# Sixteen tokens' expert rows gathered for the first expert product of a mixture layer

## The chip, the cores and the metric

The kernel runs on one core of a Trainium2 chip. The metric is the device time of one execution in microseconds (us), as the median of several runs. The engines are TensorE (PE; its weight loads are listed as PEld), VectorE (DVE), ScalarE (ACT), GpSimd (POOL) and SyncE (SP), which here issues nearly all transfers. Each engine works through its own queue in order.

## The reference

The whole is a network of four layers on 256 tokens of width 1024, in float32: two layers with attention, convolution and a gated FFN, one with an mLSTM mixer, one with stick-breaking attention. The last two each end in the expert layer (`peer_ffn`), which is what the change touches:

```
q = xb @ w_q                                  # 8 heads x 2 halves x 128
s = q . sub_keys; s_top, i_top = top_k(s, 16) # 128 keys per half
cand = all 16 x 16 sums; g_top, pos = top_k(cand, 16)
expert = i_top[0][..] * 128 + i_top[1][..]    # 16 of 16384 experts per head and token
act = gelu(einsum('thkd,td->thk', take(peer_u, expert), xb))
out = einsum('thk,thkd->td', softmax(g_top) * act, take(peer_v, expert))
```

`peer_u` and `peer_v` are 16384 x 1024 each, per layer. A token uses 128 of the 16384 experts. Its input is xb = normalised x times (1 + scale) plus shift.

## The kernel before

**Split products.** Every large product is made of three matmuls in a reduced float32 format. A weight of 128 x 1024 is loaded by SP (`raw`, four buffers), rounded by ScalarE (`whi`, L177), and the remainder is made by VectorE or POOL (`wlo`, L180); `whi` and `wlo` have five buffers each. `mm3` (L185 to L187) multiplies hi by hi, hi by lo and lo by hi.

**The expert layer** (`peer`, L896) is computed densely. The 16384 experts are 128 chunks of 128, and there are two products per chunk. `up(c)` multiplies a chunk of `peer_u` with the activations h (1024 x 256, one column per token): 8 x 3 = 24 matmuls of 256 columns into `pA`, then a Gelu by ScalarE (L920) into a table of activations. `down(c)` multiplies the weighted activations with a chunk of `peer_v`: 12 matmuls of 512 columns into `acc`. Between them `weigh` (L954) multiplies the table by each token's routing weights: it builds one-hot tables on VectorE (L961, L962, L967) and forms the dense weights by 16 f16 matmuls of 64 columns (`pG`, L971) for eight tokens and half of the chunks, and VectorE multiplies these into the table (L979).

**The order of the work.** Chunks 0 to 63 of `up` carry the routing beside them (`route`): for each of two blocks of 128 tokens first eight steps of top 16 among the keys, then four among the candidates, then four groups of one-hot operations (L1130, L1133, L1135; two of each) that look up the chosen keys. In chunks with c divisible by 3 (22 per layer) POOL makes the lo half, in the others VectorE. Chunks 64 to 99 of `up` carry `weigh` for the first half of the chunks; the last 28 chunks of `up` alternate with the first 28 of `down`, the next `down` chunks carry the other half of `weigh`, and the rest run alone. The order within an engine is set when the program is built: a scheduler puts the instructions in order by the written sequence, by data and by constraints that the code sets, such as `issue_after`, which holds a piece of work until a named instruction has been placed.

**What the layer's stream x does meanwhile.** Two tiles `x[0]` and `x[1]` of 128 x 1024 hold the network's residual stream in SBUF. In the expert layer they are only needed at its end, where `gated_x` adds the result to them. The tile `xa1` of a normalised block is free after the activations are transposed, and holds `wr`, the split activations of `down`.

## Time and profile before

| | |
|---|---|
| median of 3 runs | 2894.22 us (2889.6 to 2897.99) |
| the profiled execution | 2893.22 us, span 2891.4 us |
| mean granted TensorE clock | 0.996 of full speed |
| busy, share of the span | PE 98%, PEld 89%, DVE 75%, ACT 50%, POOL 5% |
| transfers | 543.42 MB, mean 188 GB/s |

The two expert layers start their first `up` chunk at 1093.6 us and 2095.6 us of the span. A busy engine in the profile executes or holds an instruction; matmuls are pipelined, so what counts for TensorE is the distance between starts, not the duration of one. The bracket at the end of a timeline row is the idle time before it and what ended it; where a wait is for several things, the one that came last by the profile is named.

### The profile page before, as it was taken

The numbers are of one execution on the slowest core, as the hardware profiler recorded it, in microseconds if no ns is written. First come the engines' busy times: TensorE is split into PE (matmuls) and PEld (weight loads), VectorE is DVE, ScalarE is ACT, GpSimd is POOL, SyncE is SP. The second block draws the span as 40 slices with busy tenths as digits, with TensorE's granted clock in tenths as the row PEclk, the third lists the DMA queues.
The fourth block names the chain that finished last, engine by engine and source line by source line (L and its number), as shares of the span: only waits on it lengthen the run. The fifth ranks groups of instructions, "written<-read, shape, count | busy, mean of one in ns | idle before, by whom it ended". The sixth has DMA issues, their size and how long they took to land.

```text
span 2891.4 us, 50436 instructions
## 1 busy us (share of the span) xinstructions
PE 2846.0 (98%) x19669; PEld 2575.9 (89%) x19669; DVE 2168.8 (75%) x4178; ACT 1442.9 (50%) x2372; POOL 144.2 (5%) x54
## 2 busy tenths in 40 slices
PE   8999999999999999999999999999999999999999
PEld 7998997999997889989999887877899999988887
DVE  6986766886755859968866997686599787569865
ACT  6645445654545854443344344567544434443454
POOL 0000000000000003320000000000033100000000
PEclk9999999999999999999999999999999999999999
DMA  6485775376666455554687358653455545554564
GB/s 210 135 280 191 265 247 190 111 250 221 235 192 186 161 169 163 173 197 139 196 279 254 117 193 284 217 180 101 146 163 182 170 139 166 186 165 131 186 201 146
DMA packets 153713, 543.42 MB, mean 188 GB/s; under 512 B 20018, under 2 KB 21250, under 8 KB 153346
## 3 DMA queue, kind: packets, MB, share of 16 engines
q1 hardware_dynamic: 153474, 540.20, 57.9%
q8 instruction: 154, 2.52, 0.4%
q14 instruction: 85, 0.70, 0.1%
HBM read 539.04 MB, written 1.09 MB: 187 GB/s over the span
## 4 chain that ended last, share of the span: by engine, by line
PE 86%; DVE 11%; ACT 1%; DMA 1%; issue 1%; SPq 0%; DVEq 0%; ACTq 0%
PE acc L185 8%; PE acc L187 8%; PE acc L186 8%; PE mmB L185 7%; PE mmB L186 7%; PE mmB L187 7%; PE pA L185 5%; PE pA L186 5%; PE pA L187 5%; PE mmA L185 5%; PE mmA L186 5%; PE mmA L187 5%; PE pG L971 4%; DVE wlo L180 3%; PE sc L193 1%
## 5 line engine op out<-in xcount | busy, mean ns | idle before, releaser
L177 ACT CAST whi<-raw 128x1024 fp32r<-128x1024 f32 x893 | 935.8, 1050 | 872.1 <-PE pA L186 358.2
L180 DVE TENSOR_TENSOR wlo<-raw,whi 128x1024 fp32r<-128x1024 f32 x849 | 1049.7, 1241 | 344.3 <-ACT whi L177 341.0
L185 PE MATMUL pA<-hhi,whi 128*128 128x256 f32 x2048 | 586.7, 286 | 10.6 <-ACT act L920 9.5
L186 PE MATMUL pA<-hlo,whi 128*128 128x256 f32 x2048 | 579.8, 283 | 0.0
L187 PE MATMUL pA<-hhi,wlo 128*128 128x256 f32 x2048 | 579.6, 283 | 0.0
L185 PE MATMUL mmB<-hhi,whi 128*128 128x256 f32 x1480 | 422.0, 285 | 0.0
L186 PE MATMUL mmB<-hlo,whi 128*128 128x256 f32 x1480 | 420.2, 284 | 0.0
L187 PE MATMUL mmB<-hhi,wlo 128*128 128x256 f32 x1480 | 419.9, 284 | 0.0
L185 PEld LDWEIGHTS pA<-hhi,whi 128*128 128x128 f32 x2048 | 394.2, 192 | 15.1 <-ACT act L920 11.4
L187 PE MATMUL acc<-whi,wr 128*128 128x512 f32 x1024 | 400.4, 391 | 0.8 <-DVE wr L992 0.5
L186 PE MATMUL acc<-wlo,wr 128*128 128x512 f32 x1024 | 401.0, 392 | 0.0
L186 PEld LDWEIGHTS pA<-hlo,whi 128*128 128x128 f32 x2048 | 393.1, 192 | 2.2
L185 PE MATMUL acc<-whi,wr 128*128 128x512 f32 x1024 | 393.2, 396 | 0.0
L187 PEld LDWEIGHTS pA<-hhi,wlo 128*128 128x128 f32 x2048 | 392.8, 192 | 0.0
L185 PEld LDWEIGHTS mmB<-hhi,whi 128*128 128x128 f32 x1480 | 282.8, 191 | 1.8
L187 PEld LDWEIGHTS mmB<-hhi,wlo 128*128 128x128 f32 x1480 | 282.8, 191 | 0.6
L186 PEld LDWEIGHTS mmB<-hlo,whi 128*128 128x128 f32 x1480 | 282.9, 191 | 0.5
L991 ACT CAST wr<-act 128x256 fp32r<-128x256 f32 x256 | 103.5, 406 | 343.7 <-PE acc L186 338.3
L187 PEld LDWEIGHTS acc<-whi,wr 128*128 128x128 f32 x1024 | 192.3, 188 | 44.9 <-DVE wr L992 4.8
L186 PEld LDWEIGHTS acc<-wlo,wr 128*128 128x128 f32 x1024 | 192.6, 188 | 39.2 <-DVE wlo L180 0.6
L185 PEld LDWEIGHTS acc<-whi,wr 128*128 128x128 f32 x1024 | 193.1, 189 | 35.7
L542 DVE CUSTOM_DVE_ANT_0 adaw<-adaw,cb 128x1024 f32<-128x1024 f32 x112 | 136.8, 1222 | 78.4 <-DMA adaw<-in_ada_w 74.7
(353 smaller groups left out, 4037.4 us busy)
## 6 DMA issues: line engine op xcount, KB each, us to landing
raw<-in_peer_u SPq DMA_DIRECT2D x256, 512.0 KB, 3.8
raw<-in_peer_v SPq DMA_DIRECT2D x256, 512.0 KB, 4.3
adaw<-in_ada_w SPq DMA_DIRECT2D x96, 512.0 KB, 4.5
raw<-in_w_gates SPq DMA_DIRECT2D x80, 512.0 KB, 3.7
raw<-in_w_down SPq DMA_DIRECT2D x44, 512.0 KB, 4.0
raw<-in_w_gate SPq DMA_DIRECT2D x36, 512.0 KB, 3.8
raw<-in_w_up SPq DMA_DIRECT2D x36, 512.0 KB, 3.8
raw<-in_w_qkv SPq DMA_DIRECT2D x24, 512.0 KB, 4.5
```

Of the source, the lines that this page charges most:

```text
L177: (nc.vector.tensor_copy if FIRST_HI[i:i + 1] == "v" else nc.scalar.copy)(hi, raw)
L180: self.last_lo = lo_eng.tensor_tensor(lo, raw, hi.bitcast(F32), op=ALU.subtract)
L185: nc.tensor.matmul(out, lhsT=lhs[0], rhs=rhs[0], start=start, stop=False)
L186: nc.tensor.matmul(out, lhsT=lhs[0], rhs=rhs[1], start=False, stop=False)
L187: return nc.tensor.matmul(out, lhsT=lhs[1], rhs=rhs[0], start=False, stop=stop)
L193: self.nc.tensor.matmul(out, lhsT=lhs[a], rhs=rhs[b], start=start and i == 0, stop=stop and i == 2)
L542: nc.vector.tensor_tensor_reduce(w, w, self.csilu, 1.0, 0.0, op0=ALU.mult, op1=ALU.add, accum_out=col[:, j:j + 1])
L971: nc.tensor.matmul(pg[:, :, 4 * g + t], lhsT=e2[:, g, :, t], rhs=e1[:, j, :, t], start=(j == 0), stop=(j == 1))
L991: nc.scalar.copy(gh, row(c))
```

## The change

The first `TG` = 16 tokens are left out of the dense first product: `up` runs on 240 columns. For these tokens the 128 expert rows of each token are gathered from `peer_u` (given a second time as plain rows, `peer_u_rows`) by 16 indirect transfers per layer, issued by POOL into `x[0]` and `x[1]` in turn, 128 rows of 4 KB each: gather j fetches one expert for each of 8 groups of 16 tokens' places. VectorE multiplies a gathered tile with `xg` (the 16 tokens' activations repeated eight times, with the shift added) and sums along the row (`dot`). After the last one the results are turned, passed through Gelu, multiplied by the routing weights, transposed and split into three bf16 parts `gP`; in `weigh` the own tokens use `gP` in place of the routing weights (24 matmuls instead of 16), and ScalarE writes the result where the others multiply it into the table.

x is saved to two DRAM tiles before, and read back at chunk 97 of `down`. The sixteen gathers are due at chunks 32, 35, 39, 42, 46, 49, 53, 56, 60, 63, 67, 70, 74, 77, 81 and 84, the dot of each three chunks later. The own tokens' `weigh` is last among the calls for the first half. NA falls from 100 to 98, so 30 chunks of `up` and `down` alternate. The one-hot lookups of the routing are made in f16 with the heads last: four groups per layer of six operations, the widest over 2048 elements, instead of eight.

```diff
-        N1, NA, FIN, GATE, TAIL = 64, 100, 58, 110, 4
+        N1, NA, FIN, GATE, TAIL = 64, 98, 58, 110, 4
+        G0, G1 = 32, 88
...
             def up(c, dst, lo_eng=None):
                 w = self.split_w(d["peer_u"][l, c], lo_eng=lo_eng)
-                p = self.pa.tile([128, S], F32, tag="sc", name="pA")
+                p = self.pa.tile([128, S - TG], F32, tag="sc", name="pA")
                 for k in range(KD):
-                    mm = self.mm3(p, [v[:, k * 128:(k + 1) * 128] for v in w], [v[:, k, :] for v in h],
+                    mm = self.mm3(p, [v[:, k * 128:(k + 1) * 128] for v in w], [v[:, k, TG:S] for v in h],
                                   k == 0, k == KD - 1)
-                return mm, nc.scalar.activation(dst, p, AF.Gelu)
+                return mm, nc.scalar.activation(dst[:, TG:S], p, AF.Gelu)
+
+            xd = [self.dram.tile([128, D], F32, name=f"xd{t}{l}") for t in range(NT)]
+
+            def gather_setup():
+                xg = self.np.tile([128, D], F32, tag="xa1", name="xg")
+                nc.sync.dma_start(xg, shift)
+                for t in range(NT):
+                    nc.sync.dma_start(xd[t], self.x[t])
+                fg = self.x[0]
+                for g in range(NG):
+                    nc.sync.dma_start(fg[g * TG:(g + 1) * TG, :], norm.xa[0][0:TG, :])
+                nc.vector.tensor_tensor(xg, xg, fg, op=ALU.add)
+                return xg
+
+            def gather_places():
...
+                nc.vector.tensor_scalar(eu, gw[:, 0], float(l * 16384), None, op0=ALU.add)
+                for g in range(NG):
+                    nc.sync.dma_start(gidx[g * TG:(g + 1) * TG, :], eu[:, g * TG:(g + 1) * TG])
+
+            def gather(j):
+                r = self.x[j % 2]
+                nc.gpsimd.indirect_dma_start(out=r, out_offset=None, in_=d["peer_u_rows"],
+                                             in_offset=bass.IndirectOffsetOnAxis(ap=gidx[:, j:j + 1], axis=0))
+                return r
+
+            def dot(j, r):
+                nc.vector.tensor_tensor_reduce(r, r, xg, 1.0, 0.0, op0=ALU.mult, op1=ALU.add,
+                                               accum_out=dots[:, j:j + 1])
+
+            def gather_end():
...
+                p = self.pt.tile([128, TG], F32, tag="tp", name="tpg")
+                nc.tensor.transpose(p, gw[:, 0], self.ident[0:TG, 0:TG])
...
+            for j in range(TG):
+                turn.setdefault(G0 + j * (G1 - G0) // TG, []).append(j)
+
+            def gathers(c):
+                if c == G0 - 4:
+                    assert pks
+                    gather_places()
+                for j in turn.get(c - 3, ()):
+                    with tc.issue_after(self.last_lo.ins):
+                        dot(j, got.pop(j))
+                for j in turn.get(c, ()):
+                    assert len(got) < 2
+                    got[j] = gather(j)
+                if c == G1 + 2:
+                    assert not got
+                    gather_end()
...
             for c in range(64):
                 mark = up(c, act1[:, c, :], nc.gpsimd if c % 3 == 0 else nc.vector)
...
+                if c == 4:
+                    xg = gather_setup()
+                gathers(c)
...
             for c in range(64, NA):
                 up(c, row(c), nc.vector)
-                while done < 32 and done * (NA - 65) < (c - 63) * 32:
-                    weigh(0, 8 * done)
+                gathers(c)
+                while done < 32 and done * (NA - 65) < (c - 63) * 32 and (done < (S - TG) // 8 or c >= NA - 3):
+                    weigh(0, (8 * done + TG) % S)
                     done += 1
...
-            for hg in range(4):
-                hs = slice(2 * hg, 2 * hg + 2)
-                oh = [B.tile([128, 2, 16, 16], F32, tag=f"oh{i}", name="oh") for i in range(2)]
-                for i in range(2):
-                    nc.vector.tensor_tensor(oh[i], bc(af[:, i, hs, :, None], [128, 2, 16, 16]),
-                                            bc(io16[:, None, None, :], [128, 2, 16, 16]), op=ALU.is_equal)
-                for i in range(2):
-                    nc.vector.tensor_tensor(oh[i], oh[i], bc(fi[:, hs, i, None, :], [128, 2, 16, 16]), op=ALU.mult)
-                for i in range(2):
-                    nc.vector.tensor_reduce(pk[:, i, hs, :], oh[i], axis=AX.X, op=ALU.add)
+            for i in range(2):
+                oh = B.tile([128, 16, 16, 8], F16, tag="oh", name="oh")
+                nc.vector.tensor_tensor(oh, bc(af[:, i, None], [128, 16, 16, 8]),
+                                        bc(self.iota8[:, :, None, :], [128, 16, 16, 8]), op=ALU.is_equal)
+                nc.vector.tensor_tensor(oh, oh, bc(fi[:, i, :, None, :], [128, 16, 16, 8]), op=ALU.mult)
+                for n in (8, 4, 2):
+                    nc.vector.tensor_tensor(oh[:, 0:n], oh[:, 0:n], oh[:, n:2 * n], op=ALU.add)
+                nc.vector.tensor_tensor(pk[:, i].rearrange("p h s -> p s h"), oh[:, 0], oh[:, 1], op=ALU.add)
                 yield 3.6
```

What the scheduler makes of it shows in two queues. The numbers at the names are those of buffers or of tiles, and `[waits ...]` are the semaphores that an instruction waits for: DMASW0 to DMASW7 count the gathers by turns, DMAHW the transfers of SP. VectorE's queue in the first expert layer, before, around chunks 36 and 37 (the lo half of chunk 35 is `wlo_13671`, that of 37 `wlo_13747`; that of 36 is POOL's):

```order
L180 TENSOR_TENSOR wlo_13671<-raw_13668,whi_13670 128x1024 [waits DMAHW4_49,PE_49,Activation_49]
L1049 MAX v_13390<-sc1_11712 128x8 x2
L1051 MAX_INDEX iu_13391<-v_13390,sc1_11712 128x8 [waits DVE_49] x2
L1053 MATCH_REPLACE sa_13700<-v_13390,sc1_11712 128x128
L1053 MATCH_REPLACE sa_13701<-v_13390,sc1_11712 128x128
L1055 MAX v_13390<-sa_13700 128x8 [waits DVE_49]
```

And the same place after (the lo half of chunk 35 is `wlo_13732`, of 37 `wlo_13798`, of 38 `wlo_13846`, of 40 `wlo_13912`; L960 is `dot`, whose second row reads the sum out):

```order
L183 TENSOR_TENSOR wlo_13732<-raw_13729,whi_13731 128x1024 [waits DMAHW6_49,PE_49,Activation_49]
L960 ISA x0_89,dots_11705<-x0_89,xg_12485 128x1024 [waits DMASW0_49]
L960 ISA dots_11705 128x1
L960 ISA x0_89,dots_11705<-x0_89,xg_12485 128x1024 [waits DMASW2_49]
L960 ISA dots_11705 128x1
L183 TENSOR_TENSOR wlo_13798<-raw_13795,whi_13797 128x1024 [waits DMAHW0_49,PE_49,Activation_49]
...
L183 TENSOR_TENSOR wlo_13846<-raw_13843,whi_13845 128x1024 [waits DMAHW1_49,PE_49,Activation_49]
L960 ISA x1_97,dots_11705<-x1_97,xg_12485 128x1024 [waits DMASW1_49]
L960 ISA dots_11705 128x1
L960 ISA x1_97,dots_11705<-x1_97,xg_12485 128x1024 [waits DMASW4_49]
L960 ISA dots_11705 128x1
L183 TENSOR_TENSOR wlo_13912<-raw_13909,whi_13911 128x1024 [waits DMAHW3_49,PE_49,Activation_49]
```

Between two lo halves there now stand two dots on the same tile, `x0` and then `x1`, each waiting for its own gather. POOL's whole queue, before, from the broadcasts of the first two layers on, holds one row of 22 lo halves for each expert layer:

```order
L292 TENSOR_SCALAR gb<-gb 128x1024 x4
L180 TENSOR_TENSOR wlo<-raw,whi 128x1024 x22
L774 MEMSET svz_21365 128x2048
L774 MEMSET svz_21366 128x2048
L180 TENSOR_TENSOR wlo<-raw,whi 128x1024 x22
```

and after, from the lo half of chunk 21 (`wlo_13137`) to that of chunk 42 (`wlo_14005`):

```order
L183 TENSOR_TENSOR wlo_13137<-raw_13134,whi_13136 128x1024 [waits PE_49,DMAHW0_49,Activation_49,Pool_49]
L955 DMA x0_89<-in_peer_u_rows,gidx_11704 128x1024 [waits DMAHW4_49,DMAHW5_49,DMAHW3_49,DMAHW6_49,DMAHW2_49,DMAHW7_49,DMAHW1_49,DMAHW0_49]
L955 DMA x1_97<-in_peer_u_rows,gidx_11704 128x1024
L183 TENSOR_TENSOR wlo_13248<-raw_13245,whi_13247 128x1024 [waits PE_49,Activation_49,Pool_49]
L183 TENSOR_TENSOR wlo_13380<-raw_13377,whi_13379 128x1024 [waits PE_49,DMAHW6_49,Activation_49,Pool_49]
L183 TENSOR_TENSOR wlo_13511<-raw_13508,whi_13510 128x1024 [waits PE_49,DMAHW1_49,Activation_49,Pool_49]
L183 TENSOR_TENSOR wlo_13652<-raw_13649,whi_13651 128x1024 [waits PE_49,DMAHW4_49,Activation_49,Pool_49]
L955 DMA x0_89<-in_peer_u_rows,gidx_11704 128x1024 [waits DVE_49] x2
L183 TENSOR_TENSOR wlo_13766<-raw_13763,whi_13765 128x1024 [waits PE_49,DMAHW7_49,Activation_49,Pool_49]
L955 DMA x1_97<-in_peer_u_rows,gidx_11704 128x1024 [waits DVE_49] x2
L183 TENSOR_TENSOR wlo_13879<-raw_13876,whi_13878 128x1024 [waits PE_49,DMAHW2_49,Activation_49,Pool_49]
L183 TENSOR_TENSOR wlo_14005<-raw_14002,whi_14004 128x1024 [waits PE_49,DMAHW5_49,Activation_49,Pool_49]
```

The first gathers into each tile stand ahead of the lo half of chunk 24; two more into `x0`, each waiting for VectorE, stand ahead of that of chunk 36 (`wlo_13766`), and two more into `x1` ahead of that of chunk 39. The second expert layer has the same pattern.

## Rows read from the trace of the kernel before

**Rows 1.** The page: busy us (share) xinstructions, then the chain of waits.

```profile
...
PE 2846.0 (98%) x19669; PEld 2575.9 (89%) x19669; DVE 2168.8 (75%) x4178; ACT 1442.9 (50%) x2372; POOL 144.2 (5%) x54
...
PE 86%; DVE 11%; ACT 1%; DMA 1%; issue 1%; SPq 0%; DVEq 0%; ACTq 0%
```

**Rows 2.** Windows, second expert layer: stretch, length, busy us by engine, PEclk, DMA.

```profile
...
2037.00:2095.60 58.60, 56.96 (x424) 53.21 (x424) 28.21 (x44) 32.71 (x62) 4.78 (x2) 1.00 0.51 161
2095.60:2143.00 47.40, 47.39 (x393) 47.31 (x394) 47.40 (x211) 22.75 (x33) 14.76 (x5) 1.00 0.50 154
...
2188.00:2237.00 49.00, 47.17 (x391) 46.74 (x389) 48.93 (x149) 20.82 (x31) 13.55 (x5) 1.00 0.54 181
2237.00:2284.60 47.60, 47.08 (x390) 46.82 (x391) 31.17 (x47) 25.79 (x42) 15.53 (x5) 1.00 0.61 196
...
2330.00:2376.00 46.00, 46.00 (x466) 45.53 (x465) 39.97 (x68) 16.04 (x24) 0.00 (x0) 1.00 0.45 138
```

**Rows 3.** Timeline of TensorE: start, duration, engine, line, operation, tiles, count.

```profile
...
1550.25 0.39 PE L187 MATMUL acc<-whi,wr 128*128 128x512 f32 x1
...
1552.30 0.39 PE L187 MATMUL acc<-whi,wr 128*128 128x512 f32 x1
...
1552.64 0.28 PE L186 MATMUL pA<-hlo,whi 128*128 128x256 f32 x1
...
1553.48 0.28 PE L187 MATMUL pA<-hhi,wlo 128*128 128x256 f32 x1
```

**Rows 4.** Timeline, all engines, at chunk 48, second expert layer; [idle before].

```profile
...
2233.32 1.28 DVE L1130 TENSOR_TENSOR oh<-af,iota 128x512 f32<-128x512 f32 x2
...
2236.08 1.04 ACT L177 CAST whi<-raw 128x1024 fp32r<-128x1024 f32 x1 [5.13 <-DMA raw<-in_peer_u]
2236.92 1.21 DVE L180 TENSOR_TENSOR wlo<-raw,whi 128x1024 fp32r<-128x1024 f32 x1
...
2237.46 0.19 PEld L185 LDWEIGHTS pA<-hhi,whi 128*128 128x128 f32 x1 [2.26 <-ACT act L920]
2237.46 0.39 PE L185 MATMUL pA<-hhi,whi 128*128 128x256 f32 x1 [2.06 <-ACT act L920]
```

**Rows 5.** Timeline of weight loads, eight of the scores in one row.

```profile
1052.35 0.97 PEld L1088 LDWEIGHTS pss<-sk,q 128*128 128x128 f32 x8 [0.15 <-ACT q L1075]
```

**Rows 6.** VectorE's instructions by shape: count, busy us, mean ns, idle before.

```profile
...
L542 DVE CUSTOM_DVE_ANT_0 adaw<-adaw,cb 128x1024 f32<-128x1024 f32 x112 | 136.8, 1222 | 78.4 <-DMA adaw<-in_ada_w 74.7 <-DMA adaw<-in_kv_ada_w 3.3
...
L961 DVE TENSOR_TENSOR e<-iota,slots 128x1024 f16<-128x1024 f16 x128 | 87.4, 683 | 1.5 <-ACT slots L1154 1.5
L962 DVE TENSOR_TENSOR e<-iota,slots 128x512 f16<-128x512 f16 x128 | 53.2, 417 | 0.0
...
L1133 DVE TENSOR_TENSOR oh<-oh,fi 128x512 f32<-128x512 f32 x32 | 31.6, 1025 | 0.0
```

**Rows 7.** POOL's lo halves by shape, 1095 to 1285.

```profile
...
L180 POOL TENSOR_TENSOR wlo<-raw,whi 128x1024 fp32r<-128x1024 f32 x20 | 59.3, 2966 | 126.4 <-ACT whi L177 112.9 <-PE pA L186 13.6
```

**Rows 8.** Issues of transfers: KB each, median us to landing.

```profile
...
raw<-in_peer_u SPq DMA_DIRECT2D x256, 512.0 KB, 3.8
...
ab<-rowsd SPq DMA_DIRECT2D x5, 512.0 KB, 5.5
cb<-in_c SPq DMA_DIRECT2D x2, 512.0 KB, 7.4
```

**Rows 9.** Windows around an idle stretch of TensorE, first expert layer.

```profile
...
1256.00:1260.70 4.70, 0.00 (x0) 0.00 (x0) 1.23 (x2) 2.77 (x4) 0.00 (x0) 0.65 0.82 324
1260.70:1263.00 2.30, 2.29 (x10) 2.29 (x11) 1.38 (x2) 2.11 (x3) 0.00 (x0) 0.50 0.59 173
1263.00:1265.00 2.00, 2.00 (x14) 2.00 (x14) 1.91 (x2) 0.00 (x0) 0.00 (x0) 0.70 0.68 195
```

**Rows 10.** Timeline of TensorE, one chunk of the `weigh` stage.

```profile
...
2288.49 0.36 PE L185 MATMUL pA<-hhi,whi 128*128 128x256 f32 x1
...
2292.41 0.36 PE L185 MATMUL pA<-hhi,whi 128*128 128x256 f32 x1
```

More of the change, by code (lines that the diff above doesn't have):

```diff
@@ L904, in peer @@
             h = norm.h
-            wr = self.np.tile([128, 2, 2, S], F32R, tag="xa1", name="wr")
-            slots = P(ctx, "pea").tile([128, 4, S], F16, name="slots")
+            EA = P(ctx, "pea")
+            slots = EA.tile([128, 4, S], F16, name="slots")
+            gidx = EA.tile([128, TG], U32, name="gidx")
+            dots = EA.tile([128, TG], F32, name="dots")
+            gw = EA.tile([TG, 2, 128], F32, name="gw")
+            gP = EA.tile([128, 3, TG], BF16, name="gP")
             wI, wP = slots[:, 0:2], slots[:, 2:4]
@@ new lines, in gather @@
+            def gather(j):
[7 more added lines that the diff above has]
+            def gather_end():
+                for g in range(NG):
+                    nc.sync.dma_start(gw[:, 0, g * TG:(g + 1) * TG], dots[g * TG:(g + 1) * TG, :])
+                nc.scalar.activation(gw[:, 0], gw[:, 0], AF.Gelu)
+                nc.vector.tensor_tensor(gw[:, 0], gw[:, 0], gw[:, 1], op=ALU.mult)
+                p = self.pt.tile([128, TG], F32, tag="tp", name="tpg")
+                nc.tensor.transpose(p, gw[:, 0], self.ident[0:TG, 0:TG])
+                r = dots
+                nc.scalar.copy(r, p)
+                for j in range(3):
+                    nc.vector.tensor_copy(gP[:, j], r)
+                    if j < 2:
+                        nc.vector.tensor_tensor(r, r, gP[:, j], op=ALU.subtract)
@@ L925, in spare @@
                     self.pop()
-            steps, ends = self.route(rctx, l, sc, wI, wP)
+            steps, ends, pks = self.route(rctx, l, sc, wI, wP)
             took = 0
+            got = {}
+            turn = {}
+            for j in range(TG):
[13 more added lines that the diff above has]
+                    gather_end()
             for c in range(64):
@@ L956, in weigh @@
                 pg = self.pt.tile([128, 64, 8], F32, tag="tp", name="pG")
-                e2 = B.tile([128, 2, 128, 4], F16, tag="e2", name="e2")
-                e0 = B.tile([128, 2, 64, 4], F16, tag="e0", name="e0")
+                own = t0 < TG
+                dt = BF16 if own else F16
+                parts = [gP[:, j] for j in range(3)] if own else [wP[:, j] for j in range(2)]
+                e2 = B.tile([128, 2, 128, 4], dt, tag="e2", name="e2")
+                e0 = B.tile([128, 2, 64, 4], dt, tag="e0", name="e0")
                 tg = lambda a, n: bc(a.rearrange("p (g t) -> p g t", t=4)[:, :, None, :], [128, 2, n, 4])
@@ L978, in weigh @@
                     v = tl[:, r0:r0 + i1 - i0, t0:t0 + 8]
-                    nc.vector.scalar_tensor_tensor(v, pg[:, i0:i1, :], 1.0 / WSCALE, v, op0=ALU.mult, op1=ALU.mult)
+                    if own:
+                        nc.scalar.activation(v, pg[:, i0:i1, :], AF.Copy, scale=1.0 / WSCALE)
+                    else:
+                        nc.vector.scalar_tensor_tensor(v, pg[:, i0:i1, :], 1.0 / WSCALE, v, op0=ALU.mult, op1=ALU.mult)
             acc = []
@@ L1027, in peer @@
                     C = P(ctx, "pec", 2)
+                    for t in range(NT):
+                        nc.sync.dma_start(self.x[t], xd[t])
                 if c == GATE:
@@ L1162, in route @@
         pks = []
-        return (u for t in range(NT) for u in start(t)), [lambda t=t: end(t, pks[t]) for t in range(NT)]
+        return (u for t in range(NT) for u in start(t)), [lambda t=t: end(t, pks[t]) for t in range(NT)], pks
 def layout(inp):
@@ L1309, in body @@
     kv = ada.pop(1)
-    norms += [Late(0, ada[0], 0), Late(2, ada[0], 24), Late(4, kv, 0), Late(7, ada[1], 24)]
+    norms += [Late(0, ada[0], 0), Late(2, ada[0], 24), Late(5, kv, 0), Late(8, ada[1], 24)]
     net.first_layer(1, norms[1], norms[2])
@@ L1314, in body @@
     net.bg = later
-    net.peer(0, norms[3], lambda: row(3), norms[4])
+    net.peer(0, norms[3], lambda: row(3), norms[4], row(4))
     assert not net.bg
-    net.shared_kv_sb(norms[4], (row(5), ada[1][:, 0:KD]), row(6), norms[5])
-    net.peer(1, norms[5], lambda: row(8), None, out)
+    net.shared_kv_sb(norms[4], (row(6), ada[1][:, 0:KD]), row(7), norms[5])
+    net.peer(1, norms[5], lambda: row(9), None, row(10), out)
 def kernel(**inputs):
```

51 lines of the change are left out of this document (32 added, 19 removed).

## Prediction

> **What bounds the kernel now.** I read the page first: TensorE is busy for 2846.0 us of a span of 2891.4 and holds 86% of the chain of waits, VectorE is busy 75% of the span and holds 11% of the chain [rows 1]. An average hides the stages, so next came the stretches of the second expert layer [rows 2]. In the first 48 chunks, while the routing runs, VectorE is busy for 47.40 of 47.40 us at their start and 48.93 of 49.00 at their end: it is full, and TensorE with 47.39 and 47.17 waits little yet. From chunk 48 (2237 us) on, VectorE has room (31.17 of 47.60), and in the stage with `weigh` it is at 39.97 of 46.00 while TensorE is at 46.00 of 46.00. So TensorE sets the pace from chunk 48, and VectorE before it. Third came the spacing of the matmuls in the timeline [rows 3]: nine steps of 512 columns take 2.05 us, 228 ns each; seven steps of 256 columns take 0.84 us, 120 ns each. A chunk's 24 matmuls are therefore 2.88 us. Last, how a late VectorE reaches TensorE [rows 4]: VectorE puts a one-hot group (2233.32 to 2236.92) ahead of a lo half; the raw buffers come free by lo halves, so ScalarE's cast at 2236.08 has waited 5.13 us for a raw load, the Gelu behind it is late, and TensorE has waited 2.06 us for that Gelu at 2237.46. There is no slack for more VectorE work, or VectorE waiting, ahead of chunk 48.
>
> All that follows is per expert layer, of which there are two, against the profiled execution of 2893.2 us (1.0 below the median of 2894.2).
>
> **The gain: 240 columns.** From 228 ns and 120 ns a column costs (228 - 120)/256 = 0.42 ns, so 16 columns less are 6.7 ns, a step of 113.3 ns, and 24 of them save 0.16 us a chunk. It counts only where TensorE sets the pace: chunks 48 to 127, 80 x 0.16 = **-12.9 us**. Narrow f32 steps have one neighbour: eight products of 128 columns load their weights in 0.97 us [rows 5] with 0.19 us for one [rows 4], (0.97 - 0.19)/7 = 111 ns a step though they have half the columns. So the weight load, or whatever else sets that floor, would allow 113; the saving is bounded by 9 ns at best (0.22 us a chunk) and by nothing at worst, a step that stays at 120.
>
> The Trainium skill's page "TensorE: Matmul & The Clock Gate" (section on the back-to-back issue gap) says that in a stream of weight load and matmul pairs the spacing is set by both operations, not by the columns alone. The rows here bear out a floor of 111 ns at 128 columns, but contradict its sustained figure for 512 columns (about 131 ns; here 228). By its rule a step near the floor need not shrink, which is the third rival below.
>
> **VectorE's work up to chunk 47.** Before, five of the eight one-hot groups stand ahead of that chunk's lo half, at 3.60 us each (2233.32 to 2236.92) [rows 4], 18.0 us. After, four groups of f16 operations replace the eight, and all four stand ahead of it. For an f16 operation of 2048 elements there is no row; 512 and 1024 elements take 417 and 683 ns busy [rows 6], so each doubling adds about as much again: 1.2 us for 2048, and two of these with the halving adds come to about 3.6 us a group, 14.4. Bounds: 2.4 us a group if the wide ones run at half of that, 5 us if the wide strides cost as f32 does. New are four dot products: the nearest row is the 128x1024 multiply with accumulation of the ada stage, 1222 ns [rows 6], 1.3 us each with the read of the sum, 5.2. Sum -18.0 + 14.4 + 5.2 + 0.4 for the index arithmetic (two operations of 128 elements, each below the 417 ns for 512) = +2.0; VectorE's operations stretch beside POOL's (the one-hot products take 1025 ns on average [rows 6], while a whole group of six can end in 3.60 [rows 4]), so **+2.3** (-3 to +8). The other three groups that go stood after chunk 47, where VectorE has room, and are worth nothing.
>
> **The gathers: two full latencies on VectorE.** In VectorE's order two dots on the same buffer stand back to back after the lo half of chunk 35, and two more after that of chunk 38. The second of a pair reads a gather that overwrites what the first one reads, so POOL can issue it only when the first dot is done, and the second waits out the whole transfer while VectorE stands still. Behind it in VectorE's queue are the lo half of chunk 37 and the routing; on POOL, behind a third gather that waits for the second dot, is the lo half of chunk 36 that TensorE needs next. Nothing covers this: VectorE was full there. No gather by indices is in the trace. The nearest rows are transfers of 512 KB: 3.8 us for an expert chunk, 5.5 for the rows read back from DRAM, 7.4 for a slow one [rows 8]. I take 5.5, since a gather reads 128 scattered rows, not one block: 2 x 5.5 = **+11.0** (7.6 to 14.8). A third pair stands before chunk 58, where VectorE has had ten chunks of room (31.17 of 47.60), and is taken as hidden; uncovered it would be 5.5 more.
>
> The Trainium skill's page "DMA: Bandwidth & Descriptors" (anatomy of one DMA on the GpSimd path) gives 2.0 us plus the bytes at 436 GB/s, an estimate of 3.2 us for such a gather. No run here shows it; by that the two waits would be 6.4 instead of 11.0 and the whole forecast 9 us lower.
>
> **The clock.** After TensorE had stood still for 4.7 us and more it was granted 0.50 (1.2 of 2.4 GHz) and the next 24 matmuls took 4.3 us instead of 2.88 [rows 9]. The waits above leave gaps of that kind (a gather, a dot, and POOL's 3.0 us [rows 7] for chunk 36 or 39). One of the two falls where VectorE is late anyway: **+1.6** (0 to 3.2).
>
> **Smaller terms.** SP's eight small index transfers wait for VectorE ahead of the raw loads of chunks 25 on, four buffers deep: **+1.0** (0 to 3). A chunk of the `weigh` stage takes 3.92 us (2288.49 to 2292.41) [rows 10], in which VectorE has 3.41 us of work (39.97 of 46.00) [rows 2]; TensorE's part falls to 3.76, and seven dots over 24 chunks add 9.1 us against 24 x 0.35 = 8.4 of room: **+1.0** (0 to 3). The own tokens take 24 instead of 16 matmuls of 64 columns in four `weigh` calls; sixteen take 3.92 - 2.88 = 1.04 us, so 32 x 65 ns = **+2.1**. The own tokens' `weigh` waits for the last gathers at the turn to `down`: **+1.0** (0 to 3). Saving x to DRAM, loading xg and adding it stand in the stretch before chunk 0, where VectorE is busy 28.21 of 58.60 and the transfer engines 0.51 of it, and x comes back long before the end: 0 (without that cover up to 4 us).
>
> **Sum.** Per layer -12.9 + 2.3 + 11.0 + 1.6 + 1.0 + 1.0 + 2.1 + 1.0 = +7.1; for two, +14.2, or 2907. The forecast is **2907 us**, slower. With its costs near their ends, the case itself spans 2897 to 2922.
>
> **Rivals.**
> 1. *VectorE's routing becomes cheap enough to pay for short waits: faster.* With f16 groups of 2.4 us VectorE's sum by chunk 47 is -2.8 instead of +2.0, and with gathers of 3.8 us and no clock loss a layer comes to -12.9 - 2.8 + 7.6 + 2.1 + 1.0 = -5.0, in all 2883. If nothing stalled at all, TensorE would set the pace in all 128 chunks: -20.6 + 4 a layer, 2860. For it: f16 operations of 512 elements take 417 ns, the f32 products of the one-hot groups 1025 [rows 6]. Against it: the second dot of a pair cannot start earlier than the end of the first plus a transfer, however early the first is.
> 2. *Both halves cancel.* With 3.8 us a gather, no clock loss and the small terms at zero: -12.9 + 2.3 + 7.6 + 2.1 = -0.9 a layer, 2891. Only the shortest row for 512 KB speaks for it.
> 3. *The 240-column step stays at 120 ns.* The change then does not do what it says: 2 x 12.9 more, 2933. For it is the floor at 111 ns, against it that 113 is still above that floor.
> 4. *Products of fewer than 256 columns run at a lower rate in this number format.* No such row exists here in the format of the split weights; the 128-column f32 step of 111 ns speaks against it. At half the rate a step would be some 214 ns (12 + 2 x 101), 24 x 256 x 94 ns = +577 us.
>
> **How the numbers follow.** Forecast 0.41, rival 1 0.24, rival 2 0.23, rival 3 0.10, rival 4 0.02. About 0.3% (8.7 us) is what a measurement of this kernel can tell from no change. Faster by that is rival 1, 0.24; within it rival 2, 0.23; slower the forecast with rivals 3 and 4, 0.53. For 8 in 10 the range leaves out the lower third of rival 1, the upper half of rival 3, the tail of the forecast, and rival 4: 2872 to 2936.
>
> **What would show it.** In the profile after: pA steps of 113 ns; `x0<-in_peer_u_rows` landing 5 to 6 us after its issue; two idle stretches of VectorE of some 5 us released by a DMA within chunks 35 to 40 of each layer, and TensorE waiting there at a lo half of POOL's; chunk 48 starting about 157 us after chunk 0 (before: 2237.46 - 2095.6 = 141.9); chunks of 3.76 us in the `weigh` stage (before 3.92), and 5.46 where up and down alternate (before 2.88 and twelve steps of 228 ns, 5.62). The forecast is wrong if chunk 48 comes at less than 145 us after chunk 0, if the step is 120 ns, or if the `weigh` stage turns to VectorE's pace.

## The result: 3123 us, 7.9% slower, and the profile after

| | before | after |
|---|---|---|
| median (lowest to highest of 4 runs each, same chip) | 2893.72 us (2889.6 to 2897.99) | 3123.34 us (3117.56 to 3125.41) |
| ratio, 95% interval | | 1.0794 [1.0781, 1.0807] |
| span of the profiled execution, mean granted clock | 2891.4 us, 0.996 | 3123.6 us, 0.965 |

The sign was forecast, the size (+14 us) was not: the change costs +230 us. The page of the changed kernel, to be held beside [rows 1]:

```profile
span 3123.6 us, 50831 instructions
...
PE 2886.3 (92%) x19735; PEld 2591.6 (83%) x19735; DVE 2196.4 (70%) x4237; ACT 1443.3 (46%) x2388; POOL 162.2 (5%) x86
...
PE 71%; DVE 12%; DMA 9%; issue 4%; ACT 2%; SPq 1%; POOL 1%; DVEq 0%; ACTq 0%; POOLq 0%
```

VectorE is busy for 28 us more and TensorE for 40 (in the stretch below alone it is busy 50 us longer for the same matmuls, beside a granted clock of 0.82), but no engine is fuller than before. What has grown is the part of the chain that is no engine's work: DMA from 1% to 9%, issue from 1% to 4%. That points to queues that wait for each other. The windows say where. The rows read as in [rows 2]; first the start of the second layer and its `weigh` stage, then chunks 98 to 127 of the first and of the second layer, which hold the same work but for the ada product, VectorE's product with a transferred tile of weights of the next modulation (`adaw`), which only the first has:

```profile
2296.56:2355.60 59.04, 54.94 (x479) 54.05 (x480) 58.80 (x221) 26.59 (x40) 17.27 (x6) 1.00 0.46 150
...
2528.00:2575.00 47.00, 47.00 (x508) 46.62 (x507) 46.63 (x83) 17.25 (x26) 3.75 (x4) 1.00 0.59 176
...
1489.00:1787.00 298.00, 206.43 (x1045) 174.38 (x1044) 111.45 (x149) 77.08 (x116) 0.00 (x0) 0.82 0.46 148
2655.40:2812.00 156.60, 156.60 (x1046) 143.08 (x1045) 83.41 (x87) 77.59 (x117) 0.00 (x0) 1.00 0.64 195
```

298.00 against 156.60 us for the same matmuls: 141 us are lost in this one stretch, in which no engine is full. The rest shows in how late a chunk starts. The table gives, for the first / second layer, the start of a chunk counted from that layer's chunk 0, less the same in the kernel before (us). From chunk 64 to 100 some 5 us come into it that the end of the layer gives back, since `weigh` ends and `down` starts two chunks earlier (2.8 of them by chunk 98 in e7). Chunk 48 starts 172.8 / 173.2 us after chunk 0; the forecast had 157.

| kernel | c=24 | c=40 | c=48 | c=64 | c=98 | c=127 |
|---|---|---|---|---|---|---|
| after | 11.8 / 12.5 | 29.6 / 29.6 | 31.4 / 31.3 | 46.3 / 36.7 | 66.4 / 38.7 | 204.1 / 35.0 |
| ada product put back (e1) | 10.9 / 11.7 | 28.3 / 28.9 | 31.8 / 30.9 | 46.2 / 37.2 | 49.3 / 40.8 | 45.6 / 37.1 |
| three mends (e4) | 6.0 / 5.9 | 11.4 / 11.2 | 17.4 / 17.6 | 29.4 / 19.4 | 30.9 / 23.0 | 27.2 / 19.3 |
| routing alone (e7) | 2.4 / 2.2 | 3.9 / 3.6 | 5.8 / 5.0 | 0.6 / 4.9 | 3.4 / 7.8 | 6.1 / 10.4 |
| change with 256 columns (e11) | 2.6 / 2.3 | 6.6 / 6.4 | 8.8 / 9.3 | 4.8 / 9.4 | 9.5 / 14.1 | 12.2 / 16.7 |
| all mended (e10) | 3.2 / 0.9 | 1.2 / -1.2 | 1.8 / -0.9 | 3.5 / 2.1 | 8.1 / 1.6 | 4.4 / -2.1 |

**The loop in the first layer.** The timeline of the changed kernel, one turn in chunks 98 to 127 (SPq is the issue of a transfer):

```profile
1586.04 1.23 DVE L545 CUSTOM_DVE_ANT_0 adaw<-adaw,cb 128x1024 f32<-128x1024 f32 x1 [6.94 <-DMA adaw<-in_ada_w]
...
1587.62 1.23 DVE L183 TENSOR_TENSOR wlo<-raw,whi 128x1024 fp32r<-128x1024 f32 x1
...
1588.87 0.33 SPq L169 DMA_DIRECT2D raw<-in_peer_v  x1
...
1590.34 0.33 SPq L169 DMA_DIRECT2D raw<-in_peer_u  x1
...
1590.72 0.43 SPq L544 DMA_DIRECT2D adaw<-in_ada_w  x1
...
1597.27 1.23 DVE L545 CUSTOM_DVE_ANT_0 adaw<-adaw,cb 128x1024 f32<-128x1024 f32 x1 [6.96 <-DMA adaw<-in_ada_w]
```

And the same place in the kernel before:

```profile
1441.49 1.23 DVE L180 TENSOR_TENSOR wlo<-raw,whi 128x1024 fp32r<-128x1024 f32 x1 [0.53 <-ACT whi L177]
...
1442.75 0.33 SPq L166 DMA_DIRECT2D raw<-in_peer_u  x1
1442.99 1.23 DVE L542 CUSTOM_DVE_ANT_0 adaw<-adaw,cb 128x1024 f32<-128x1024 f32 x1 [0.27 <-DMA adaw<-in_ada_w]
...
1444.17 1.22 DVE L180 TENSOR_TENSOR wlo<-raw,whi 128x1024 fp32r<-128x1024 f32 x1
1444.25 0.33 SPq L541 DMA_DIRECT2D adaw<-in_ada_w  x1
```

In both, the product waits for its tile of `adaw`, the next transfer into that tile is issued only after the product, and its issue stands in SP's queue behind two raw loads. Before, the lo half that frees the second raw buffer is done when the product's turn comes (lo half at 1441.49, raw at 1442.75, product at 1442.99, next transfer at 1444.25, beside the work). After, the product stands two lo halves, a whole turn, earlier in VectorE's queue, ahead of both lo halves that free the buffers. Counted through both queues from their start: the next transfer stands behind raw load 463 in either kernel, and with four buffers that load needs lo half 459. The product ahead of this transfer stands behind lo half 459 in the kernel before (at 1489.26) and behind 457 now (at 1608.34). So one turn is: product 1586.04, lo halves, raw issues at 1588.87 and 1590.34, `adaw` issue only then at 1590.72, and 6.5 us later the next product. Two in-order queues wait for each other in a ring, 11 us a turn instead of the 5.4 of the second layer. TensorE's granted clock falls to 0.82 on average beside it.

**The index transfers and the pairs.** Chunk 22, first layer:

```profile
1154.15 0.33 SPq L169 DMA_DIRECT2D raw<-in_peer_u  x1
...
1159.02 5.17 SPq L951 DMA_DIRECT2D gidx<-eu  x8
...
1164.29 8.27 SPq L169 DMA_DIRECT2D raw<-in_peer_u  x5
...
1168.04 1.04 ACT L180 CAST whi<-raw 128x1024 fp32r<-128x1024 f32 x1 [8.91 <-DMA raw<-in_peer_u]
...
1169.41 0.57 PE L188 MATMUL pA<-hhi,whi 128*128 128x240 f32 x1 [7.28 <-ACT act L929]
```

SP issues a raw load at 1154.15, waits for the indices from VectorE, and then eight transfers of 1 KB hold it for 5.17 us; the raw load behind them, that of chunk 25, is issued only at 1164.29. ScalarE's cast waits 8.91 us for it. Behind that cast in ScalarE's queue stands the Gelu of chunk 20, which frees the buffer for chunk 22, so TensorE waits 7.28 us there. Chunk 36, the first pair of dots on one tile:

```profile
1208.39 1.22 DVE L960 CUSTOM_DVE_ANT_0 x<-x,xg 128x1024 f32<-128x1024 f32 x1
...
1209.89 0.95 POOL L955 DMA_INDIRECT x<-in_peer_u_rows,gidx  x1 [14.64 <-DVE dots L960]
...
1214.63 1.23 DVE L960 CUSTOM_DVE_ANT_0 x<-x,xg 128x1024 f32<-128x1024 f32 x1 [5.01 <-DMA x<-in_peer_u_rows,gidx]
...
1216.13 1.68 POOL L955 DMA_INDIRECT x<-in_peer_u_rows,gidx  x1 [5.30 <-DVE dots L960]
...
1217.83 2.35 POOL L183 TENSOR_TENSOR wlo<-raw,whi 128x1024 fp32r<-128x1024 f32 x1
...
1220.23 0.57 PE L190 MATMUL pA<-hhi,wlo 128*128 128x240 f32 x1 [6.30 <-POOL wlo L183]
```

This is the forecast chain, link by link: the first dot releases POOL's gather, the second dot waits 5.01 us for it, POOL's lo half follows the third gather, and TensorE waits 6.30 us for it.

**Steps of TensorE**, against [rows 3] and [rows 10]: 20 steps of 240 columns, then two chunks of the `weigh` stage.

```profile
2297.00 0.27 PE L188 MATMUL pA<-hhi,whi 128*128 128x240 f32 x1
...
2299.23 0.27 PE L190 MATMUL pA<-hhi,wlo 128*128 128x240 f32 x1
...
2540.88 0.36 PE L188 MATMUL pA<-hhi,whi 128*128 128x240 f32 x1
...
2544.61 0.36 PE L188 MATMUL pA<-hhi,whi 128*128 128x240 f32 x1
```

(2299.23 - 2297.00)/20 = 111.5 ns a step, and 3.73 us a chunk: the narrower product does what it says.

### The profile page after: what moved, and what is told of

Read it like the earlier page. It is cut to its first block, busy times and chain, and to the rows that moved or that the text cites. A ratio compares the mean times of both kernels' runs of the same rounds, so it can differ in the third digit from the quotient of the medians.

```text
span 3123.6 us, 50831 instructions
## 1 busy us (share of the span) xinstructions
PE 2886.3 (92%) x19735; PEld 2591.6 (83%) x19735; DVE 2196.4 (70%) x4237; ACT 1443.3 (46%) x2388; POOL 162.2 (5%) x86
## 4 chain that ended last, share of the span: by engine, by line
PE 71%; DVE 12%; DMA 9%; issue 4%; ACT 2%; SPq 1%; POOL 1%; DVEq 0%; ACTq 0%; POOLq 0%
PE acc L188 7%; PE acc L190 7%; PE acc L189 7%; PE mmB L188 6%; PE mmB L189 6%; PE mmB L190 6%; DMA adaw<-in_ada_w 6%; DVE wlo L183 5%; PE mmA L189 4%; PE mmA L188 4%; PE mmA L190 4%; PE pG L1058 4%; PE pA L188 4%; PE pA L189 4%; PE pA L190 4%
## 5 line engine op out<-in xcount | busy, mean ns | idle before, releaser
L188 PE MATMUL pA<-hhi,whi 128*128 128x240 f32 x2048 | 582.7, 285 | 52.7 <-ACT act L929 51.6
L190 PE MATMUL pA<-hhi,wlo 128*128 128x240 f32 x2048 | 574.2, 280 | 27.6 <-POOL wlo L183 25.3
L189 PE MATMUL pA<-hlo,whi 128*128 128x240 f32 x2048 | 573.3, 280 | 0.0
L189 PE MATMUL acc<-wlo,wr 128*128 128x512 f32 x1024 | 422.5, 413 | 91.6 <-DVE wlo L183 91.6
L188 PEld LDWEIGHTS pA<-hhi,whi 128*128 128x128 f32 x2048 | 402.5, 197 | 62.5 <-ACT act L929 57.8
L190 PEld LDWEIGHTS pA<-hhi,wlo 128*128 128x128 f32 x2048 | 400.0, 195 | 29.2 <-POOL wlo L183 26.2
L190 PE MATMUL acc<-whi,wr 128*128 128x512 f32 x1024 | 418.0, 408 | 0.7 <-DVE wr L1082 0.6
L189 PEld LDWEIGHTS pA<-hlo,whi 128*128 128x128 f32 x2048 | 400.2, 195 | 13.8 <-issue 10.8
L188 PE MATMUL acc<-whi,wr 128*128 128x512 f32 x1024 | 405.5, 409 | 0.0
L189 PEld LDWEIGHTS acc<-wlo,wr 128*128 128x128 f32 x1024 | 201.6, 197 | 142.0 <-DVE wlo L183 100.5
L190 PEld LDWEIGHTS acc<-whi,wr 128*128 128x128 f32 x1024 | 202.0, 197 | 47.1 <-DVE wr L1082 3.6
L188 PEld LDWEIGHTS acc<-whi,wr 128*128 128x128 f32 x1024 | 201.4, 197 | 36.2
```

The source lines that it names most:

```text
L188: nc.tensor.matmul(out, lhsT=lhs[0], rhs=rhs[0], start=start, stop=False)
L189: nc.tensor.matmul(out, lhsT=lhs[0], rhs=rhs[1], start=False, stop=False)
L190: return nc.tensor.matmul(out, lhsT=lhs[1], rhs=rhs[0], start=False, stop=stop)
```

## The experiments

**e1: the ada product behind the lo half again.** One constraint in the alternating chunks of the changed kernel puts it back where it stood before.

```diff
 for c in range(LAG):
+    before = self.last_lo.ins
     down(c)
     up(NA + c, row(NA + c), nc.vector)
-    spare(True)
+    with tc.issue_after(before):
+        spare(True)
```

> One thing is put back as before: in the stretch of the first expert layer where up and down alternate, VectorE's product with a block of the ada weights stands behind the lo half of the previous turn again, one turn later than in the changed kernel. Theory (a loop between two queues): in the changed kernel the product stands right behind the lo half that frees the raw buffer for the load that is ahead of the ada transfer in SP's queue, so each turn is transfer + product + two lo halves in series, 10.9 us instead of 5.4 for some 26 turns. Then this kernel takes 3123 - 26 x 5.5 = 2980 us or a little less (2955 to 2990). Rival (the transfers themselves are slower, by the reload of x and the gathers): the turns stay near 10 us and the time above 3090.

Measured 2967.4 us (2964.69 to 2968.87), ratio to before 1.0259 [1.0242, 1.0276]: 156 us less than the changed kernel. Chunks 98 to 127 of the first layer:

```profile
1471.10:1627.70 156.60, 156.60 (x1046) 143.05 (x1045) 110.81 (x148) 77.65 (x117) 0.00 (x0) 1.00 0.84 281
```

156.60 us instead of 298.00, TensorE without a gap, the clock at 1.00. Some 18 us more came back in chunks 92 to 97 of that layer, where the product had also waited for its transfer at the head of VectorE's queue. Two thirds of the loss hang on the place of one unchanged instruction of each turn.

**e2: index transfers behind a raw load that is already due.** `+ with tc.issue_after(self.last_dma.ins):` around the eight.

> The eight small transfers of the indices stand behind the raw load of chunk 28 in SP's queue, not in front of that of chunk 25. Theory (SP's queue is blocked by them: the raw load behind was issued 10 us after the one ahead): the stall of TensorE of 7.3 us at chunk 22 and the slow chunk behind it go in both layers, 2 x 10 us, so 3103 us (3098 to 3110). Rival (the stall comes from POOL, whose first gathers hold up its lo halves): no change, 3118 to 3128, with the stall at another chunk.

3114.1 us (3108.24 to 3118.4), 1.0765 [1.0746, 1.0785]: 9 us less than the changed kernel, half of what was expected. Chunk 24 is then 3.5 / 2.7 late instead of 11.8 / 12.5, but chunk 36 again 8.8 / 6.8: between them VectorE is full (36.00 us of 1160 to 1196), and the loads' earlier arrival is of little use there. Some 4.5 us a layer are left at chunk 48.

**e3: dots behind a lo half of VectorE's own.** `issue_after` holds the work back on the queue of the named instruction only. For the dots due at chunks 42, 45 and 63 the newest lo half is POOL's, so on VectorE's queue they were free to move up, and stood behind an earlier dot.

```diff
+        if lo_eng is nc.vector:
+            self.dve_lo = self.last_lo
...
-                    with tc.issue_after(self.last_lo.ins):
+                    with tc.issue_after(self.dve_lo.ins):
                         dot(j, got.pop(j))
```

> Each dot is queued behind the last lo half that VectorE made, where the changed kernel names the last lo half of either engine: dots 2, 3 and 8 fall on chunks whose lo half is POOL's, so nothing held them back on VectorE and each moved up to the dot before it on the same tile. Theory (the three pairs cost a gather's latency each, and POOL's lo half behind it): the stalls at chunks 36, 39 and 57 to 59, 26 us in the second layer and 32 in the first, shrink to a few us; with VectorE full before chunk 48 about a third is given back later: 3123 - 40 = 3083 us (3065 to 3095). Rival (it is VectorE's work that is too much before chunk 48, not the waits): less than 10 us, above 3113.

3095.5 us (3093.62 to 3103.19), 1.071 [1.069, 1.073]: 28 us less, just short of the range that was expected (up to 3095). All three pairs are gone: VectorE's dots wait for nothing (idle 0.0 us over 32 of them, after the change 30.0).

**e4: all three.**

> The three edits together. Theory: the losses lie in separate stretches and add up, 3123 - 143 - 20 - 40 = 2920 us (2890 to 2930), with chunk 48 starting at most 150 us after chunk 0 in both layers. Rival (with one wait gone the next takes its place, above all POOL's lo halves behind gathers that wait for dots): 2935 or more, and chunk 48 at over 158 us.

2929.67 us (2926.08 to 2932.55), 1.0131 [1.0114, 1.0148]: 194 us less, and 156 + 9 + 28 = 193, so the three add up. But chunk 48 comes 159 us after chunk 0, not 150, and chunk 59 of the second layer takes 8.12 us:

```profile
2305.27 0.60 PE L1248 MATMUL tpr<-ident,pk 128*128 128x128 f32 x4
...
2306.69 1.28 ACT L1240 ACT_TABLE_LOAD   x1
...
2308.32 0.49 DVE L1242 TENSOR_REDUCE gsum<-pk 128x8 f32<-128x128 f32 x2 [2.15 <-ACT pk L1240]
...
2310.18 0.69 PE L1248 MATMUL tpr<-ident,pk 128*128 128x128 f32 x2 [3.42 <-DVE pk L1245]
```

TensorE transposes the routing's results (`tpr`); the last two transposes wait for the softmax on ScalarE and VectorE, with the rest of the chunk behind them. In the kernel before they stood 31 rows behind the first four in TensorE's queue, here 9.

**e5: those two transposes one chunk later**, the `end` of the routing cut in two (`left = [end() for end in ends]`, then `go()` at `c == FIN + 1`).

> As the run with the three edits (2929.7 us), and the end of the routing in two parts: the transposes that need no softmax after chunk 58, those that do after chunk 59. In the changed kernel and in the run with three edits they stand six matmuls into chunk 59 in TensorE's queue, and chunk 59 takes 8.1 us in the second layer and 15.3 in the first instead of 2.7; before, they stood one chunk later and cost 0.8 us. Theory (TensorE waits there for the softmax, which waits for ScalarE's table): 17 us less, 2913 us (2907 to 2921). Rival (the stall is that of VectorE or of the transfers of the ada block, and the transposes only show it): 2925 or more.

2925.32 us (2924.6 to 2927.5), 1.0114 [1.0099, 1.013]: only 4 us less than e4, and the two intervals overlap: nearer to the rival. Chunk 59 still takes 10.85 / 4.89 us and in the first layer chunk 60 now 5.25 (normal is 2.68).

**e6: gathers from chunk 48 on, routing at a slower pace** (`G0, G1 = 48, 88`; `took < 1.45 * (c + 1)` instead of 1.7; `gather_end` behind the newest lo half and load).

> As the run before it, and: the gathers at chunks 48 to 85 instead of 32 to 84; the routing paced at 1.45 instead of 1.7 units a chunk, so that its shorter work ends near chunk 54 as before, not at 47; the last steps of the gathers (eight transfers, Gelu, product) queued behind the lo half and the raw load of chunk 90. Theory (VectorE was over its time before chunk 48 by dots and by routing work moved forward, and TensorE's 240 columns are worth 0.2 us a chunk wherever VectorE keeps up): nearly all of 256 x 0.2 = 51 us comes through, less 4 for the own tokens and some 10 of stalls: 2855 us (2840 to 2875), and chunk 48 starts 135 us after chunk 0 or less. Rival (VectorE is full in the weigh stage too: 3.41 us of work and 0.5 of dots against 3.74 a chunk): 2885 or more, with chunks above 3.74 there.

2917.83 us (2914.8 to 2922.09), 1.0092 [1.0076, 1.0107]: the theory was wrong by more than 60 us. Chunk 40 is now early (-1.0 / -1.3), but the eight index transfers, now behind the raw load of chunk 44, hold SP for 5.0 / 5.7 us again and chunk 44 is 9.3 / 9.9 late. A VectorE that has room was not enough.

**e7: the new routing alone**: the kernel before with the f16 one-hots and NA = 98, no gathers, 256 columns.

> The kernel before with one part of the change: the one-hot lookups in f16, four groups instead of eight at the same pace, and NA 98 for the room. Theory of the prediction (four groups of 3.6 us instead of five ahead of chunk 47, the three others hidden anyway): chunk 48 starts 0 to 4 us earlier in each layer, the whole within 2884 to 2893. Rival (the shorter work moves forward, so VectorE is late sooner, around chunk 22): chunk 24 starts 3 us or more later than before, and the whole is no faster, 2890 to 2900.

2898.52 us (2893.92 to 2903.94, 11 runs), 1.0022 [1.0013, 1.0031]: 6 us slower, as the rival had it, though chunk 24 is only 2.4 / 2.2 us late where the rival had 3. The group of one-hots in the changed kernel's trace:

```profile
1154.03 1.21 DVE L1221 TENSOR_TENSOR oh<-af,iota 128x2048 f16<-128x2048 f16 x1
...
1155.28 1.23 DVE L1223 TENSOR_TENSOR oh<-oh,fi 128x2048 f16<-128x2048 f16 x1
...
1156.54 1.48 DVE L1225 TENSOR_TENSOR oh<-oh 128x1024 f16<-128x1024 f16 x3
...
1158.05 0.37 DVE L1226 TENSOR_TENSOR pk<-oh 128x128 f32<-128x128 f16 x1
```

From 1154.03 to 1158.42 it takes 4.4 us, not 3.6; four groups are 17.6 us ahead of chunk 48, as much as the five old ones (18.0). That by itself would make no difference, but chunk 48 comes 5 us later. What fits is the rival's reason: up to chunk 36 VectorE does 132.4 / 133.2 us of work in e7 (durations added up) and 127.5 / 127.3 before, and chunk 36 is 4.4 / 3.9 late; by chunk 48 it has done less than before (167.2 / 168.7 against 170.7 / 170.2) and stood idle for 3 to 4 us, but the delay stays. The shorter work has moved forward, to where VectorE is full.

**e8: e5 with the indices through DRAM in two transfers** instead of eight.

> As the run with the softmax split (2925.3 us), but the indices go to their 128 places in two transfers by way of DRAM instead of eight small ones. Theory (with eight, SP's queue stands for 5.2 to 5.7 us because a later one waits for an earlier one to land, and every raw load behind is late by that, with VectorE full): chunk 28 starts 3 us earlier in each layer, the whole 2919 us (2914 to 2922). Rival (it is VectorE's work in that stretch that sets the pace): within 2 us of 2925.

2925.83 us (2923.07 to 2928.47), 1.0121 [1.0104, 1.0139]: no change from e5: chunk 48 is 17.2 / 16.9 late, in e5 17.4 / 19.6. The rival's reading fits, that VectorE sets the pace ahead of chunk 48.

**e9: e6 with all mends**: e8's transfers, the ada work behind VectorE's lo half, gathers behind POOL's, the transposes at `FIN - 2` and `FIN`.

> Everything together: the spaced run (2917.8 us) with the indices and the sums in two transfers each by way of DRAM; each gather queued behind POOL's last lo half, so no lo half stands behind a gather that waits for a dot; the first half of the end of the routing at chunk 56 and its second at 58; ScalarE's and VectorE's part of the ada block queued behind the Gelu and the lo half of chunk 59 (before the change they stood at chunk 54 and cost 7 us there in the first layer). Theory (what is left are waits at the heads of queues: 10 us at chunks 41 to 43 in both layers, 20 around 52 and 59 in the first, 7 at 54 in the second, and 240 columns pay wherever none stands): 2917.8 - 2 x 10 - 20 - 7 = 2870 us (2855 to 2885). Rival (the work itself does not fit, VectorE's dots above all): above 2895.

2898.26 us (2897.15 to 2904.1, 9 runs), 1.0028 [1.0018, 1.0039]; expected was 2870, and the rival had above 2895. Chunk 48 is in time (-0.6 / 0.9), but chunks 85 and 86 take 8.7 and 6.4 us in place of 3.74:

```profile
2375.51 0.31 ACT L975 ACTIVATE gw<-gw 16x128 f32<-16x128 f32 x1 [10.45 <-DMA gw<-gwd]
2375.73 1.03 ACT L180 CAST whi<-raw 128x1024 fp32r<-128x1024 f32 x1
...
2377.07 0.57 PE L192 MATMUL pA<-hhi,whi 128*128 128x240 f32 x1 [4.73 <-ACT act L933]
```

The Gelu of 16 x 128 numbers stands at the head of ScalarE's queue 10.45 us before its transfer has landed, and the casts for TensorE stand behind it.

**e10: that Gelu two chunks behind its transfer**, the transposes one more:

```diff
+                if c == G1 + 4:
+                    with tc.issue_after(mark[1].ins), tc.issue_after(self.dve_lo.ins):
+                        gather_weights()
...
```

> The kernel of the run before with one thing more: the transfers of the 16 tokens' dots are issued after chunk 90 as there, but their Gelu and product stand behind ScalarE's and VectorE's work of chunk 92, and the transposes and parts behind that of chunk 93. Theory: in the run before the Gelu of gw stood at the head of ScalarE's queue and waited 10.45 us for its transfer, with the casts behind it, so that chunks 85 and 86 took 8.7 and 6.4 us instead of 3.74: 7.6 us in each layer. With three chunks between transfer and Gelu those come back: 2898.3 - 15 = 2883 us, range 2878 to 2889, chunk 92 less than 3 us behind its place before the change (it was 9.9 and 9.2). Rival: VectorE and the one-hots of the own tokens in chunks 95 to 97 set the time there, and the wait only moves to them: 2893 to 2899, with chunk 98 still 9 or more behind.

2886.57 us (2884.79 to 2888.75, 11 runs; before 2889.73 on the same chip), 0.9986 [0.9977, 0.9995]: 12 us less, and chunk 85 back to 3.8 / 3.9 us. So part of what e9 missed was this wait and not the work, as e9's rival had it. It beats the kernel before, by 0.14%.

**e11: the changed kernel with all 256 columns in the first product.**

```diff
-                p = self.pa.tile([128, S - TG], F32, tag="sc", name="pA")
+                p = self.pa.tile([128, S], F32, tag="sc", name="pA")
...
-                    ... [v[:, k, TG:S] for v in h], ...
+                    ... [v[:, k, 0:S] for v in h], ...
...
```

> The changed kernel with one thing undone: the first product takes all 256 columns again (the own tokens' columns are computed and then overwritten by their weights), all else, the gathers, dots and the late weigh included, as in the changed kernel. In its VectorE order the ada product of layer 0's alternating chunks stands one lo later, behind lo_u of the chunk before, as in the kernel before the change. Theory: the loop between SP's queue and VectorE's comes with the shorter turn alone, through the order; without it chunks 100 to 125 of layer 0 take 5.4 us: 3123 - 156 + 2 x (80 x 0.16) at most for the columns that come back = 2967 to 2993 us, the more of the 26 us missing the more VectorE and the queues set the turns up to chunk 64. Rival: the loop hangs on the late allocation of the wr buffer or on the own tokens' weigh and not on where the product stands: over 3100 us.

2915.2 us (2911.73 to 2916.69), 1.0089 [1.0072, 1.0106]: some 205 us less than the changed kernel (by the two ratios), and 52 below the theory's range. The kernel that multiplies more columns takes 6.5% less time. Not only the ring is gone; chunks 98 to 127 of the first layer, and the dots, with the idle time before them last:

```profile
1427.11:1590.09 162.98, 162.98 (x1045) 148.74 (x1044) 114.22 (x157) 78.02 (x117) 0.00 (x0) 1.00 0.82 277
```

```profile
L960 DVE CUSTOM_DVE_ANT_0 x<-x,xg 128x1024 f32<-128x1024 f32 x32 | 41.0, 1286 | 1.8 <-DMA x<-in_peer_u_rows,gidx 1.8
```

Chunks 98 to 127 take 162.98 us with TensorE full, and the dots wait 1.8 us in all. The same line of the changed kernel:

```profile
L960 DVE CUSTOM_DVE_ANT_0 x<-x,xg 128x1024 f32<-128x1024 f32 x32 | 41.2, 1287 | 30.0 <-DMA x<-in_peer_u_rows,gidx 30.0
```

In e11's VectorE queue lo halves stand between the dots of the first two pairs, and in SP's queue the eight index transfers stand behind four more raw loads; chunk 24 is 2.6 late, not 11.8, and chunk 40 6.6, not 29.6. Only the column count was changed: the order of the other instructions follows from it.

**e12: e10 with all 256 columns**, for what the narrower product is worth where the queues don't wait.

> The kernel of the last run (2886.6 us) with all 256 columns in the first product: the own tokens' columns are computed and then overwritten. It measures what leaving them out is worth where the queues are mended. Theory: most of 80 chunks x 0.16 us x 2 layers = 25.6 us, less what VectorE eats from chunk 24 to 48: chunk 98 of layer 1 is 8 to 13 us further behind and the time is 2886.6 + 16 to 26 = 2903 to 2912. Rival: other engines set the turns on most chunks, so that little of it is seen: below 2896, chunk 98 less than 5 us later.

2899.75 us (2897.74 to 2900.6), 1.0032 [1.0019, 1.0044] against 0.9986 of e10: 0.46%, or 13 us, less than the 16 to 26 that the theory had. From chunk 98 to 127 e10 gains 6.3 us on it in each layer (0.22 a chunk: 5.40 against 5.62 us). Up to chunk 48 of the second layer it gains nothing (-0.9 late in both), and from 48 to 98 it gains 4.3 there of 50 x 0.2 = 10; in the first layer it loses 2.3 in that stretch.

## Why the prediction was wrong

**The step that failed** is the sum's silent one: that outside the places it named, the order of the work stays as it was, so that TensorE sets the pace in chunks 48 to 127 of both layers. The prediction looked at the queues where new instructions stand, and priced each there. But the scheduler orders all instructions anew, and in chunks 98 to 127 of the first layer the ring set the pace: 10.3 us a chunk on average where 5.46 was forecast. The missing term is +156 us for the ring (e1) and, with it, most of the miss of 216; the rest is in the terms and waits below. The prediction's windows [rows 2] are of the second layer, whose alternating chunks have no ada product. A sign stood in [rows 6]: the ada products had waited 74.7 us for their transfers already before, 37.5 of them in these chunks, where they now wait 187.2.

**What was right.** *The pairs*: waits of 5.01 us against 5.5 taken, at chunks 36 and 39, with the chain through POOL as described. In the two layers the three pairs cost 28 us (e3); the forecast had 25 for two pairs. The nearness is in part luck. At chunk 40 the two pairs cost 12.6 us a layer (e3 against the changed kernel), as forecast, but at chunk 48 only 8.8 are left. And the third pair was "taken as hidden" and was not: in the second layer chunk 57 takes 6.80 us with it and 2.68 without (e3), so dots that wait 5 us hold up lo halves also where VectorE has room on average. The cause of the pairs was missed as well: not gathering as such, but a constraint that names POOL's instruction and leaves VectorE's queue free (e3). *The clock*: after the wait of 6.30 us at chunk 36 the granted clock is 0.50 (1.2 GHz) up to 1225.2, and the last 22 matmuls of the chunk take 5.0 us instead of 2.5; what of that reaches chunk 48 is not separated from the pairs. *The step*: 111.5 ns against 113.3; `weigh` 3.73 against 3.76; alternating chunks 5.40 against 5.46. Rivals 3 and 4 are refuted by it. *The own tokens' `weigh`*, +1.0 and half of +2.1: from chunk 92 to 98 e12 falls back by 3.7 us in each layer and e7, with as many columns but no own tokens, by 0.7 and 0.8; some 3 us are theirs.

**What was mis-sized.** *The index transfers*: +1.0 a layer, measured 8 to 10 (chunk 24 in e2 against after): the estimate counted four buffers as cover, and the weights of chunk 22 were indeed there. But the cast of chunk 25 stood at the head of ScalarE's queue with the Gelu of chunk 20 behind it, the chain of [rows 4]. Four loads further down the queue (e11) chunk 24 is only 2.6 late, 2.4 of it with the routing alone (e7), but chunk 28 then is 6.4 / 7.0 late against 3.4 / 2.9, so the transfers still cost 3 to 4 us there. *VectorE up to chunk 47*: routing -3.6, measured about +5 (e7). A group takes 4.4 us (taken 3.6, bounds 2.4 and 5): the two wide operations came as taken, 1.21 and 1.23 us, but the four adds take 1.9 us and not 1.2. Four groups then cost what the five old ones did, and the rest is where the work stands (e7): the sum up to chunk 47 was the wrong measure. *The gain of -12.9 a layer*: in the mended kernel 13 us for both; it is had in full only in chunks 98 to 127, where TensorE has no gap.

**What was not seen at all**: the ring between SP and VectorE, the transposes that wait for the softmax, and `gather_end` at the head of ScalarE's queue.

**Rivals 1 and 2** assumed smaller costs and fell with the rest, and no case but rival 4 had a loss above 40 us: none took up what the scheduler does to work that the change does not touch.

**What stays open.** That 240 columns change the order is shown (e11), and that this order costs 156 us by the ring (e1). Why the scheduler puts the product two lo halves earlier at 240 columns was not tried; nor is it shown which of the late chunks in the all-mended kernel (41, 60, 96) could still be had back.

## What to carry to other kernels

After any change to a program whose order a scheduler sets, compare every in-order queue over its whole length with the one before, also where nothing was edited, and look for a waiting instruction that now stands ahead of the one that frees its own transfer: in such a ring each turn is a transfer and the work in series (here 11 us for 5.4). Name, for a constraint, an instruction on the queue that is to be held. And price a saving only where its engine has no gap: of the 25.8 us that the narrower product was to bring, 13 came, and only after the queues were mended.
